# A hybrid decoder layer on one core: TensorE's order in local attention written out by hand, with three branch products moved from its end to its head

## The chip, the core and the metric

The kernel runs on one core of a Trainium2 chip. The metric is the device time of one execution in microseconds (us); the kernel before takes 1939.35 us as the median of three runs (1938.84 to 1944.86). PE is TensorE, ACT is ScalarE, DVE is VectorE, POOL is GpSimd and SP is SyncE, whose queue issues nearly all transfers of this kernel.

## The reference

One decoder layer for 1024 prompt tokens and 8 sample tokens (1032 columns in all), width 1024, in float32. Three branches are computed from one projection of the input, each is projected again by its own 1024 x 1024 matrix, and they are merged by gates:

```python
z = x @ w_in
xr, yr, q, k, v, xq, g = jnp.split(z, SPLIT_IDX, axis=-1)
a_out = hs * gelu(yr)                 # branch a: a gated linear recurrence over xr
s_out = swa_prompt(q, k, v, sinks)    # branch s: window 128, 16 query heads, 4 key/value heads of 64
c_out = mem_attn(xq, mem_k, mem_v)    # branch c: attention into 256 memory tokens
merged = sum(gates[:, :, n] * (br @ w_branch[n]) for n, br in enumerate((a_out, s_out, c_out)))
h = layer_norm(ALPHA * x + merged @ w_out, ...)
h = layer_norm(ALPHA * h + (silu(gt) * up) @ w_down, ...)
```

In `swa_prompt` the tokens lie in 8 blocks of 128. A block's queries see the keys of their own block and of the one before (the first block sees itself alone). Scores are masked to the window, a learned sink per head joins the softmax's sum, and the normalised weights multiply the values.

## The kernel before

The program is built stage by stage: the input projection, the attention into memory (`mem_attention`), local attention (`windows`), what is left of the branch projections, the output projection, the feed-forward block. This case is about `windows` (L634) and what lies at its two ends.

A float32 operand is kept as two parts, high and low, which `split` (L77) makes: ACT casts the high part (L79), DVE subtracts to get the low part (L80). A product is then three matmuls per 128 rows of contraction (`mm3`, L115: high by high, high by low, low by high).

Local attention has 32 steps, one for each of the 4 key/value heads (`kv`) and 8 blocks (`b`). Three groups of work belong to a step:

- `win_scores` (L576): eight matmuls (L594, L595) into two PSUM banks `bs`; DVE adds the mask and finds the maximum (L598), ACT takes the exponential with its sum (L602), DVE the reciprocal (L603), and DVE, POOL and ACT scale the four heads' weights (L607, L609). They lie in the tile `bp`, of which there are three.
- The first half of `win_values` (L612): PE transposes the weights into a bank `bt`, four transposes for each of the one or two key blocks (L619), and `split` makes `bph` and `bpl` of each bank.
- The second half of `win_values`: two matmuls with the values for each key block (L624, L625) into the one bank `bo`; ACT and DVE add its two halves (L629, L630), and SP stores them to the scratch tensor `scr_s` (L632).

`win_load` (L558) loads a head's keys `ks`, queries `st` and values `vs`; there are six `st` tiles for four per head, so the last two of a head take the places of the first two of the head before.

PE has work beside this: the projections of branches a and c. `branch` (L670) is a generator, and each `fill(1)` takes one *branch product* from it (L653), which is 24 matmuls into a bank `bra` or `brc`, for one of 8 row tiles and one of three column ranges c of 384, 390 and 258 columns. There are 24 products for each branch; 11 of branch a are taken in `mem_attention`. `load_branch` (L131) loads a column range of a branch from scratch and splits it; of branch s it is first called behind `windows`, since `scr_s` is what `windows` writes. The products of branch s (`brs`) come next on PE.

The order on every engine is made by a scheduler from the program's order and its own estimate of times, since `windows` writes no order down. In the program's order two products are taken ahead of the first scores, one ahead of each `win_values`, and three are left for the time behind `windows`. PE works through its queue strictly in the order that was set; so do ACT, DVE, POOL and SP with theirs.

Of the kernel before, what the change touches and what calls it, by code (L numbers as in the profile page):

```python
# [18 lines left out]
P = 128  # L19
# [42 lines left out]
class Builder:  # L62
# [546 lines left out]
                (nc.gpsimd if g else nc.vector).tensor_scalar_mul(pg[g], pg[g], r)  # L609
        return pg  # L610

    def win_values(self, kv, ops, b, pg):  # L612
        nc = self.nc
        nk, vs = len(range(max(b - 1, 0), b + 1)), ops[2]
        ov = self.bank("o", f"bo{kv}_{b}")
        for kk in range(nk):
            pt = self.bank("t", f"bt{kv}_{b}_{kk}")
            for g in range(4):
                nc.tensor.transpose(pt[:, g * P:(g + 1) * P], pg[g][:, kk * P:(kk + 1) * P], self.ident)  # L619
            hi = self.ph.tile([P, 512], F32R, tag="pt", name=f"bph{kv}_{b}_{kk}", bufs=4)  # L620
            lo = self.ph.tile([P, 512], F32R, tag="pt", name=f"bpl{kv}_{b}_{kk}", bufs=4)
            self.split(hi, lo, pt)
            v = vs[:, max(b - 1, 0) + kk, :]
            nc.tensor.matmul(ov, v, hi, start=kk == 0, stop=False)  # L624
            self.last_mm = nc.tensor.matmul(ov, v, lo, start=False, stop=kk == nk - 1).ins  # L625
        for i in range(2):
            ob = self.ph.tile([64, 256], F32, tag="ob", name=f"bob{kv}_{b}_{i}", bufs=4)
            o = ov[:, i * 256:(i + 1) * 256]
            nc.scalar.copy(ob, o[64:128, :])  # L629
            nc.vector.tensor_add(ob, o[0:64, :], ob)  # L630
            dst = self.scr["s"][:, 2 * kv + i, b * P:(b + 1) * P].rearrange("(e d) t -> d e t", e=2)
            nc.sync.dma_start(dst, ob.rearrange("p (e t) -> p e t", e=2))  # L632

    def windows(self, fill):  # L634

        self.mask = self.ph.tile([P, 256], F32, tag="mask", name="mask", bufs=1)
        self.nc.sync.dma_start(self.mask, self.io["cst"][:, P:P + 256])
        nxt, last = self.win_load(0), None
        fill(2)
        for kv in range(4):  # L640
            ops = nxt
            for b in range(8):
                pg = self.win_scores(kv, ops, b)
                if last:
                    fill(1)
                    self.win_values(*last)
                last = kv, ops, b, pg
                if b == 4 and kv < 3:
                    nxt = self.win_load(kv + 1)
        fill(1)  # L650
        self.win_values(*last)

    def product(self, step, br, m, c, wb, gate):  # L653

# [958 lines left out]
```

## Time and profile before

| what | value |
|---|---|
| median of three runs | 1939.35 us (1938.84 to 1944.86) |
| the profiled execution | 1941.62 us, of which its instructions span 1939.8 us |
| PE busy | 1902.9 us, 98% of the span |
| DVE, ACT, POOL busy | 72%, 52%, 6% |
| mean granted clock of PE | 0.995 |
| first score matmul of local attention | 825.20 us from the span's start |
| first matmul of branch s | 1046.88 us |

Times in the profile count from the start of the span. A PE instruction's duration is modelled and overlaps the next one's, so what PE really needs for a matmul is read from the distance of two starts, and a PE that is "busy" can still lose time. The names in a row read out<-in. The stage of this change is the stretch of 221.68 us between the last two times of the table.

### The profile page before, as it was taken

What the parts mean: (1) busy time and instruction counts of PE and PEld (TensorE: products, weight loads), DVE (VectorE), ACT (ScalarE), POOL (GpSimd) and SP (SyncE); (2) the same over time, 40 slices, a digit from 0 to 9 for tenths busy, and PEclk for the clock granted to TensorE, in tenths of its full rate; (3) what the DMA queues carried; (4) which work ended last, traced back from release to release, by engine and by line L of the source; (5) the groups of instructions that cost most, each with busy time, mean ns of one, the idle gap of its engine ahead of it and who ended that gap; (6) DMA issues with size and microseconds to landing.
All of it is one profiled execution on the core that took longest, in us unless ns stands there. A gap on an engine that the chain in (4) does not pass through costs nothing.

```text
span 1939.8 us, 37994 instructions
## 1 busy us (share of the span) xinstructions
PE 1902.9 (98%) x14716; PEld 1872.2 (97%) x14716; DVE 1388.3 (72%) x2738; ACT 1001.3 (52%) x2115; POOL 117.1 (6%) x168
## 2 busy tenths in 40 slices
PE   9999999999999999999999999999999999999996
PEld 9999999999999998988899999999999999999996
DVE  7878987887866655378887557785667667858467
ACT  6555565555655544388775224543433434636424
POOL 1000001110000000022210000000000000001001
PEclk9999999999999999999999999999999999999998
DMA  8545555445523376667534352123245245768542
GB/s 318 175 146 168 169 177 180 137 145 204 183 78 127 126 238 212 201 170 209 152 100 148 110 192 71 50 99 98 88 159 191 100 133 181 256 162 231 137 143 88
DMA packets 171637, 303.20 MB, mean 156 GB/s; under 512 B 19568, under 2 KB 86208, under 8 KB 171456
## 3 DMA queue, kind: packets, MB, share of 16 engines
q1 hardware_dynamic: 168384, 290.22, 45.6%
q0 software_dynamic: 3072, 10.55, 2.8%
q8 instruction: 115, 1.88, 0.4%
q14 instruction: 66, 0.54, 0.1%
HBM read 214.79 MB, written 90.09 MB: 157 GB/s over the span
## 4 chain that ended last, share of the span: by engine, by line
PE 86%; ACT 5%; DVE 4%; DMA 3%; issue 1%; ACTq 0%; SPq 0%; DVEq 0%; POOL 0%; POOLq 0%
PE ub L247 5%; PE ub L245 5%; PE ub L246 5%; PE ubfg L245 4%; PE ubfg L246 4%; PE ubfg L247 4%; PE ud L247 3%; PE ud L246 3%; PE ud L245 3%; PE udfg L245 2%; PE udfg L246 2%; PE udfg L247 2%; PE op L122 2%; PE op L120 2%; PE op L121 2%; PE brs L120 2%
## 5 line engine op out<-in xcount | busy, mean ns | idle before, releaser
L122 PE MATMUL op<-mh,wol 128*128 128x258 f32 x256 | 72.3, 282 | 1.3 <-DVE wol L80 1.3
L120 PE MATMUL op<-mh,woh 128*128 128x258 f32 x256 | 72.5, 283 | 0.0
L121 PE MATMUL op<-ml,woh 128*128 128x258 f32 x256 | 72.1, 282 | 0.0
L602 ACT ACTIVATE bp<-bp,bst 128x257 f32<-128x257 f32 (+1 forms) x128 | 62.8, 493 | 17.6 <-DVE bst L598 17.3
L245 PE MATMUL ub<-th,u_4h 128*128 128x258 f32 x240 | 67.8, 283 | 1.3 <-ACT u2s L271 1.3
L245 PE MATMUL ub<-th,u_0h 128*128 128x258 f32 x240 | 68.0, 283 | 0.6 <-ACT zb L1482 0.5
L247 PE MATMUL ub<-th,u_0l 128*128 128x258 f32 x240 | 68.2, 284 | 0.0
L247 PE MATMUL ub<-th,u_4l 128*128 128x258 f32 x240 | 68.2, 284 | 0.0
L247 PE MATMUL ub<-th,u_2l 128*128 128x258 f32 x240 | 68.2, 284 | 0.0
L247 PE MATMUL uc<-th,u_3l 128*128 128x258 f32 x240 | 68.2, 284 | 0.0
L247 PE MATMUL ud<-th,u_1l 128*128 128x258 f32 x240 | 68.2, 284 | 0.0
L247 PE MATMUL ud<-th,u_5l 128*128 128x258 f32 x240 | 68.1, 284 | 0.0
L247 PE MATMUL ub<-th,u_6l 128*128 128x258 f32 x240 | 68.1, 284 | 0.0
L245 PE MATMUL ub<-th,u_6h 128*128 128x258 f32 x240 | 68.0, 283 | 0.0
L245 PE MATMUL uc<-th,u_3h 128*128 128x258 f32 x240 | 67.9, 283 | 0.0
L245 PE MATMUL ub<-th,u_2h 128*128 128x258 f32 x240 | 67.8, 283 | 0.0
L245 PE MATMUL ud<-th,u_5h 128*128 128x258 f32 x240 | 67.8, 282 | 0.0
L245 PE MATMUL ud<-th,u_1h 128*128 128x258 f32 x240 | 67.7, 282 | 0.0
L246 PE MATMUL ub<-tl,u_6h 128*128 128x258 f32 x240 | 67.7, 282 | 0.0
L246 PE MATMUL ud<-tl,u_5h 128*128 128x258 f32 x240 | 67.7, 282 | 0.0
L246 PE MATMUL ub<-tl,u_4h 128*128 128x258 f32 x240 | 67.7, 282 | 0.0
L246 PE MATMUL ud<-tl,u_1h 128*128 128x258 f32 x240 | 67.7, 282 | 0.0
(946 smaller groups left out, 8221.9 us busy)
## 6 DMA issues: line engine op xcount, KB each, us to landing
ur<-win SPq DMA_DIRECT2D x120, 256.0 KB, 3.0
urfg<-wgu SPq DMA_DIRECT2D x80, 256.0 KB, 2.6
scr_f<-G SPq DMA_DIRECT2D x22, 516.0 KB, 3.3
f<-scr_f SPq DMA_DIRECT2D x16, 516.0 KB, 6.1
fs<-scr_t SPq DMA_DIRECT2D x16, 516.0 KB, 8.0
dck<-cmk SPq DMA_DIRECT2D x32, 256.0 KB, 3.5
dcv<-cmvT SPq DMA_DIRECT2D x32, 256.0 KB, 3.4
st<-scr_q SPq DMA_DIRECT2D x32, 256.0 KB, 5.4
```

The costliest lines, as they stand in the source:

```text
L120: nc.tensor.matmul(ps, sh, mh, start=opens and i == 0, stop=False)
L121: nc.tensor.matmul(ps, sh, ml, start=False, stop=False)
L122: self.last_mm = nc.tensor.matmul(ps, sl, mh, start=False, stop=closes and i == last).ins
L245: mm(sh[:, w], xh, start=opens and k == 0, stop=False)
L246: mm(sh[:, w], xl, start=False, stop=False)
L247: self.last_mm = mm(sl[:, w], xh, start=False, stop=k == 3).ins
L602: nc.scalar.activation(x, x, AF.Exp, bias=st[:, g:g + 1], scale=-1.0, accum_out=st[:, 4 + g:5 + g])
```

## The change

`win_values` is cut in two. Its first half becomes `win_turn` (the transposes and their splits), its second half keeps the name. `windows` runs them a step apart and writes PE's order down (`manual_schedule` for PE alone): in each step the scores of block n, the value products of block n-2, the transposes of block n-1, and one whole branch product. Five branch products are taken ahead of the first scores, where two were, so none is left behind the stage. The other engines' orders are still made by the scheduler, which now sees PE's order as given.

```diff
--- before.py
+++ after.py
@@ -609,20 +609,25 @@
                 (nc.gpsimd if g else nc.vector).tensor_scalar_mul(pg[g], pg[g], r)
         return pg
 
-    def win_values(self, kv, ops, b, pg):
-        nc = self.nc
-        nk, vs = len(range(max(b - 1, 0), b + 1)), ops[2]
-        ov = self.bank("o", f"bo{kv}_{b}")
-        for kk in range(nk):
+    def win_turn(self, kv, ops, b, pg):
+
+        out = []
+        for kk in range(2 if b else 1):
             pt = self.bank("t", f"bt{kv}_{b}_{kk}")
             for g in range(4):
-                nc.tensor.transpose(pt[:, g * P:(g + 1) * P], pg[g][:, kk * P:(kk + 1) * P], self.ident)
+                self.nc.tensor.transpose(pt[:, g * P:(g + 1) * P], pg[g][:, kk * P:(kk + 1) * P], self.ident)
             hi = self.ph.tile([P, 512], F32R, tag="pt", name=f"bph{kv}_{b}_{kk}", bufs=4)
             lo = self.ph.tile([P, 512], F32R, tag="pt", name=f"bpl{kv}_{b}_{kk}", bufs=4)
             self.split(hi, lo, pt)
-            v = vs[:, max(b - 1, 0) + kk, :]
+            out.append((ops[2][:, max(b - 1, 0) + kk, :], hi, lo))
+        return kv, b, out
+
+    def win_values(self, kv, b, terms):
+        nc = self.nc
+        ov = self.bank("o", f"bo{kv}_{b}")
+        for kk, (v, hi, lo) in enumerate(terms):
             nc.tensor.matmul(ov, v, hi, start=kk == 0, stop=False)
-            self.last_mm = nc.tensor.matmul(ov, v, lo, start=False, stop=kk == nk - 1).ins
+            self.last_mm = nc.tensor.matmul(ov, v, lo, start=False, stop=kk == len(terms) - 1).ins
         for i in range(2):
             ob = self.ph.tile([64, 256], F32, tag="ob", name=f"bob{kv}_{b}_{i}", bufs=4)
             o = ov[:, i * 256:(i + 1) * 256]
@@ -635,20 +640,25 @@
 
         self.mask = self.ph.tile([P, 256], F32, tag="mask", name="mask", bufs=1)
         self.nc.sync.dma_start(self.mask, self.io["cst"][:, P:P + 256])
-        nxt, last = self.win_load(0), None
-        fill(2)
-        for kv in range(4):
-            ops = nxt
-            for b in range(8):
-                pg = self.win_scores(kv, ops, b)
-                if last:
-                    fill(1)
-                    self.win_values(*last)
-                last = kv, ops, b, pg
-                if b == 4 and kv < 3:
-                    nxt = self.win_load(kv + 1)
-        fill(1)
-        self.win_values(*last)
+        nxt, scored, turned = self.win_load(0), None, None
+        fill(5)
+        with self.tc.manual_schedule(engines={mybir.EngineType.PE}):
+            for kv in range(4):
+                ops = nxt
+                for b in range(8):
+                    pg = self.win_scores(kv, ops, b)
+                    if turned:
+                        self.win_values(*turned)
+                    if scored:
+                        turned = self.win_turn(*scored)
+                        fill(1)
+                    scored = kv, ops, b, pg
+                    if b == 4 and kv < 3:
+                        nxt = self.win_load(kv + 1)
+            self.win_values(*turned)
+            turned = self.win_turn(*scored)
+            fill(1)
+            self.win_values(*turned)
 
     def product(self, step, br, m, c, wb, gate):
```

Every engine keeps its instructions, and their number; only their order differs. On PE it is the same up to the last three matmuls of the product `bra5_0`, and again from the first matmul of branch s.

The first place is the head of the stage on PE, where the first transposes stand (`bt0_0_0` and `bp0_0` belong to head 0, block 0; the number behind a name is the buffer's). Before:

```order
L594 MATMUL bs0_3_0_11199<-ks0_0_10929,st0_0_10935 128x256
L619 MATMUL bt0_0_0_11094<-ident_63,bp0_0_11016 128x128
L595 MATMUL bs0_3_0_11199<-ks0_1_10930,st0_0_10935 128x256
L619 MATMUL bt0_0_0_11094<-ident_63,bp0_0_11016 128x128 x2
L594 MATMUL bs0_3_0_11199<-ks0_0_10929,st0_1_10938 128x256
L619 MATMUL bt0_0_0_11094<-ident_63,bp0_0_11016 128x128
L595 MATMUL bs0_3_0_11199<-ks0_1_10930,st0_1_10938 128x256
```

Now:

```order
L594 MATMUL bs0_1_1_11145<-ks0_0_10929,st0_2_10941 128x256
L595 MATMUL bs0_1_1_11145<-ks0_1_10930,st0_2_10941 128x256
L594 MATMUL bs0_1_1_11145<-ks0_0_10929,st0_3_10944 128x256
L595 MATMUL bs0_1_1_11145<-ks0_1_10930,st0_3_10944 128x256
L618 MATMUL bt0_0_0_11161<-ident_63,bp0_0_11110 128x128 x4
L120 MATMUL bra5_1_11170<-baH0_1_9710,wba50_h_11071 128x390
L121 MATMUL bra5_1_11170<-baL0_1_9711,wba50_h_11071 128x390
L122 MATMUL bra5_1_11170<-baH0_1_9710,wba50_l_11072 128x390
```

The first transposes stood among the scores of block 3, taken apart by them; now they stand right behind the scores of block 1 and ahead of the next branch product.

The second place is the end of the stage on PE, from the last transposes or the last branch product (`brc7_2`) on; `bo3_7` is the value product of the last block, `brs0_0` the first product of branch s. Before:

```order
L619 MATMUL bt3_7_1_13949<-ident_63,bp3_7_13827 128x128 x4
L120 MATMUL brc7_0_14026<-bcH0_0_12020,wbc70_h_14016 128x384
L121 MATMUL brc7_0_14026<-bcL0_0_12021,wbc70_h_14016 128x384
L624 MATMUL bo3_7_13937<-bph3_7_0_13943,vs3_12939 128x512
L122 MATMUL brc7_0_14026<-bcH0_0_12020,wbc70_l_14017 128x384
L120 MATMUL brc7_0_14026<-bcH1_0_12023,wbc70_h_14016 128x384
L121 MATMUL brc7_0_14026<-bcL1_0_12024,wbc70_h_14016 128x384
L625 MATMUL bo3_7_13937<-bpl3_7_0_13944,vs3_12939 128x512
L624 MATMUL bo3_7_13937<-bph3_7_1_13954,vs3_12939 128x512
L122 MATMUL brc7_0_14026<-bcH1_0_12023,wbc70_l_14017 128x384
L625 MATMUL bo3_7_13937<-bpl3_7_1_13955,vs3_12939 128x512
```

Now:

```order
L120 MATMUL brc7_2_14025<-bcH7_2_12354,wbc71_h_13879 128x258
L121 MATMUL brc7_2_14025<-bcL7_2_12355,wbc71_h_13879 128x258
L122 MATMUL brc7_2_14025<-bcH7_2_12354,wbc71_l_13880 128x258
L629 MATMUL bo3_7_14052<-bph3_7_0_14012,vs3_13023 128x512
L630 MATMUL bo3_7_14052<-bpl3_7_0_14013,vs3_13023 128x512
L629 MATMUL bo3_7_14052<-bph3_7_1_14021,vs3_13023 128x512
L630 MATMUL bo3_7_14052<-bpl3_7_1_14022,vs3_13023 128x512
L120 MATMUL brs0_0_14144<-bsH0_0_14070,wbs00_h_14134 128x384
L121 MATMUL brs0_0_14144<-bsL0_0_14071,wbs00_h_14134 128x384
L122 MATMUL brs0_0_14144<-bsH0_0_14070,wbs00_l_14135 128x384
```

The last value product stood four matmuls into `brc7_0`, with the rest of that product, `brc7_1` and `brc7_2` behind it; now it is the last thing ahead of branch s.

The third place is SP's queue at the same point: the last stores of `scr_s` (from the tiles `bob3_7`), the loads of branch s (`bsL`), weight loads (`wbs`) and a gate load (`gts`, 128 x 1032). Before:

```order
L632 DMA scr_s_73<-bob3_6_1_13906 64x2x128
L680 DMA gts0_14127<-scr_g_75 128x1032
L95 DMA wbs3r1__14524<-wbr 128x512
L632 DMA scr_s_73<-bob3_7_0_13960 64x2x128
L632 DMA scr_s_73<-bob3_7_1_13964 64x2x128
L138 DMA bsL0_0_13973<-scr_s_73 128x384
L138 DMA bsL1_0_13976<-scr_s_73 128x384
```

Now:

```order
L95 DMA wbs4r0__14624<-wbr 128x512
L95 DMA wbs4r1__14630<-wbr 128x512
L637 DMA scr_s_73<-bob3_7_0_14057 64x2x128
L690 DMA gts1_14173<-scr_g_75 128x1032
L637 DMA scr_s_73<-bob3_7_1_14061 64x2x128
L138 DMA bsL0_0_14071<-scr_s_73 128x384
L138 DMA bsL1_0_14074<-scr_s_73 128x384
```

The loads of branch s stand right behind the last store in both. The gate load (now that of the next row tile, `gts1`) has moved from ahead of the last two stores to between them, and two weight loads stand ahead of both where there was one.

## The prediction

> **What bounds the kernel now.** I read the page's head first, then the stretches of the stage, then PE's instructions one by one.
>
> ```profile
> span 1939.8 us, 37994 instructions
> PE 1902.9 (98%) x14716; PEld 1872.2 (97%) x14716; DVE 1388.3 (72%) x2738; ACT 1001.3 (52%) x2115; POOL 117.1 (6%) x168
> ```
>
> PE bounds the whole span. The change moves PE's instructions and drops none, so it can give back only time that PE loses between them. The stretches of the stage (columns: length; busy time with instructions of PE, weight loads, DVE, ACT, POOL; granted clock; DMA share; GB/s):
>
> ```profile
> 825.20:836.00 10.80, 10.80 (x77) 10.80 (x77) 4.77 (x19) 3.61 (x13) 0.00 (x0) 1.00 0.99 241
> 836.00:980.00 144.00, 138.49 (x886) 126.30 (x886) 125.25 (x391) 120.34 (x365) 31.79 (x48) 1.00 0.62 173
> 980.00:1022.00 42.00, 41.71 (x273) 39.30 (x272) 33.16 (x100) 29.61 (x89) 8.64 (x13) 1.00 0.28 78
> ```
>
> PE's busy time hides its losses, because durations overlap. So I price each kind by distances of starts:
>
> ```profile
> 844.43 0.40 PE L624 MATMUL bo<-bph,vs 128*128 128x512 f32 x1
> 844.66 0.39 PE L625 MATMUL bo<-bpl,vs 128*128 128x512 f32 x1
> 844.89 0.82 PE L619 MATMUL bt<-ident,bp 128*128 128x128 f32 x6
> 845.67 0.28 PE L595 MATMUL bs<-ks,st 128*128 128x256 f32 x1
> 845.78 0.29 PE L594 MATMUL bs<-ks,st 128*128 128x256 f32 x1
> ...
> 1039.70 0.34 PE L120 MATMUL brc<-bcH,wbc_h 128*128 128x390 f32 x1
> 1043.99 0.28 PE L120 MATMUL brc<-bcH,wbc_h 128*128 128x258 f32 x1
> 1046.88 0.34 PE L120 MATMUL brs<-bsH,wbs_h 128*128 128x384 f32 x1
> 1051.04 0.34 PE L120 MATMUL brs<-bsH,wbs_h 128*128 128x384 f32 x1
> ```
>
> A value matmul takes 0.234 (844.43 to 844.89, two), a score matmul 0.118, and six transposes with one score matmul 0.78, so a transpose 0.11. A branch product of 24 matmuls takes 4.29 for 390 columns, 2.89 for 258 and 4.16 for 384. By the code the stage holds 11 products of each width less 21 matmuls of one (43 + 47 + 32 us), 224 score matmuls (26), 32 of half size (2), 240 transposes (26) and 120 value matmuls (28): 203.6 us in a stretch of 221.7. **PE loses 18.1 us here**, and that is the most the change can return. Most of it lies in 836 to 980, where DVE and ACT are busy 87% and 84% of the time. Who waited for the split weights shows the kind:
>
> ```profile
> PEld bo L624: 8.8, 26
> PE bo L624: 2.4, 5
> PEld bo L625: 1.7, 6
> ```
>
> 12.9 us were spent by value products on splits whose transposes stood only a little ahead of them.
>
> **The change part by part.** *The steady steps.* A step on PE is now scores (0.94), values (0.94), transposes (0.88) and a product: 6.9, 7.1 or 5.7 us. Between a block's transposes and its value product lie a product and a block's scores, 3.8 to 5.2 us. Two casts and two subtractions of 0.6 to 0.7 us each must fit in it beside the engine's other work, so those 12.9 us should go. DVE and ACT fit on average: in the 196.8 us of the three rows they are busy for 163 and 154. What is late next: the scores' way to the next transposes. Its length is seen at the last block, from the last score matmul to POOL's scaling:
>
> ```profile
> 1023.89 0.28 PE L595 MATMUL bs<-ks,st 128*128 128x256 f32 x1
> 1027.05 1.09 POOL L609 TENSOR_SCALAR bp<-bp,bst 128x256 f32<-128x256 f32 x1 [5.24 <-DVE bst L603]
> ```
>
> That is 4.0 us undisturbed, and the new order leaves 7.9 (6.6 where the product is the narrow one). From 836 to 980 PE stood visibly idle for 5.5 us (144.0 less 138.5), in the quieter 980 to 1022 for 0.3. For the whole interior I leave 1.5, nearer to the quiet row; bounds 0.5 and 5.5. On SP some stores now stand behind weight loads; only the four `bob` tiles wait for stores, two steps later, so I cost that at nothing (a step's length at most where two stores are late together, inside the 5.5).
>
> *The head.* The same products stand ahead of the first scores as before, but now nothing may be put between these scores and the first transposes except block 1's scores. First the loads:
>
> ```profile
> 812.75 2.64 SPq L566 DMA_DIRECT2D ks<-scr_k  x4
> 815.45 5.21 SPq L570 DMA_DIRECT2D st<-scr_q  x8
> 820.00:840.00 20.00, 20.00 (x139) 19.64 (x138) 10.26 (x41) 8.85 (x29) 1.68 (x3) 1.00 0.80 196
> DMA to landing us min/median/max: 3.7/5.4/9.6
> ```
>
> Twelve loads of 256 KB, 3.15 MB at 196 GB/s, land by about 828.4 (the last, issued by 820.7, lands between 824 and 830 by the last row, which is that of `st`). PE reaches block 0's scores at 825.7, three held-back matmuls later than before. They end at 828.5, the chain of a half-size block takes about 3 (an estimate from the 4.0), and the first transposes start near 831.3. PE has 1.4 us of scores to do in these 5.6 (some transposes start sooner): **3.9 us lost**, bounds 2.0 (loads there at once) and 5.5.
>
> *The changes of head.* The last two `st` of a head take places that are free when the last block's scores have read them. At the change from the third to the fourth head:
>
> ```profile
> 967.85 0.36 PE L594 MATMUL bs<-ks,st 128*128 128x256 f32 x1
> 968.37 2.40 SPq L570 DMA_DIRECT2D st<-scr_q  x4
> ```
>
> The fourth issue comes 2.3 us behind the scores' start and lands 5.4 later: 7.7. Before, products filled this time. Now the next scores need it when a step and two score matmuls have passed: at 7.3 and 7.1 at the first two changes, at 6.0 at the third, whose product is narrow: 0.4 + 0.6 + 1.7 = **2.7 us lost**. Bounds 0 (at 3.7 each) and 5 (weight loads stand ahead of the second pair on SP, and wait for a place of their own).
>
> *The end.* The three products that followed the last value product are gone to the head. Behind it stands a chain that they covered:
>
> ```profile
> 1036.35 0.39 PE L625 MATMUL bo<-bpl,vs 128*128 128x512 f32 x1
> 1038.03 0.42 DVE L630 TENSOR_TENSOR bob<-bo,bob 64x256 f32<-64x256 f32 x1 [0.44 <-ACT bob L629]
> 1039.15 7.54 SPq L138 DMA_DIRECT2D bsL<-scr_s  x15
> DMA to landing us min/median/max: 2.6/4.4/4.8
> 1041.77 1.00 ACT L79 CAST bsH<-bsL 128x384 fp32r<-128x384 f32 x2 [3.77 <-DMA bsL<-scr_s]
> 1042.32 0.56 DVE L80 TENSOR_TENSOR bsL<-bsL,bsH 128x384 fp32r<-128x384 f32 x1 [1.27 <-ACT bsH L79]
> 1043.83 1.01 ACT L79 CAST bsH<-bsL 128x384 fp32r<-128x384 f32 x2 [1.05 <-DMA bsL<-scr_s]
> 1040.00:1050.00 10.00, 10.00 (x66) 10.00 (x65) 7.38 (x16) 6.49 (x15) 0.00 (x0) 1.00 0.90 300
> ```
>
> From the last value matmul's end (1036.74) to the first load's issue: 2.4, with the gate load now between the last stores 2.8. The first load lands 2.6 later, its cast and subtraction take 1.05: at 6.45 the first of eight row tiles is ready. A tile is 0.197 MB: 0.66 us at the 300 GB/s of the last row, 1.03 by the casts (two at 1041.77, the third waiting until 1043.83). I take 0.75, near the bandwidth. The eighth is ready at 11.7, its three matmuls end at 12.2, and the product itself is worth 4.16: **8.1 us lost**; bounds 7.1 (at 0.66, the gate load costing nothing more) and 11.8 (at 1.03, plus its 528 KB ahead, 1.8).
>
> *The clock.* Idle PE lost its clock twice near here:
>
> ```profile
> 696.60 0.44 PE L121 MATMUL bra<-baL,wba_h 128*128 128x384 f32 x1 [2.05 <-DVE baL L80]
> 697.11:700.52 3.41, 3.41 (x13) 3.41 (x12) 3.41 (x8) 0.71 (x2) 0.00 (x0) 0.50 0.78 265
> 763.80 0.39 PE L120 MATMUL cs<-mkh,cqh 128*128 128x256 f32 x1 [1.37 <-ACT cp L507]
> 765.38:768.79 3.41, 3.41 (x14) 3.02 (x13) 3.34 (x8) 1.78 (x6) 0.00 (x0) 0.50 0.70 228
> ```
>
> After gaps of 2.05 and 1.37 us it ran at half speed for 3.41. The head's gap (two pieces of near 2 and 1) should do the same: 1.1 of the 1.7 us that this costs at most if it happens once, bounds 0 and 2. At the end the first half-speed product is paced by its loads anyway: 1.0, bounds 0 and 2.
>
> [...]
>
> **The sum.** Lost before 18.1; lost after 1.5 + 3.9 + 2.7 + 8.1 + 1.1 + 1.0 = 18.3. Net +0.2 (all lower ends together: 9.6 lost, 8.5 faster; all upper ends: 31.8, 13.7 slower). The profiled execution took 1941.62 us around its span of 1939.8, 2.3 above the median of the runs; the same +0.2 on the median 1939.35 gives **1939.6 us**. What the steps gain, the two ends take back.
>
> **The rivals.** *Slower: the vector engines can't hold the written tempo.* Before, a late block let other PE work pass; now PE stands. The nine steps from head 0, block 6 on also carry branch c's 24 casts and subtractions, on engines already busy 84 and 87% there. If casts that wait for their loads sit ahead of exponentials in ACT's queue, the way from scores to transposes grows from 4.0 past the 6.6 to 7.9 that the order leaves; from that point each further us is paid in every step. One us over in nine steps: 9 more, 1948.6. Against it: the slack of 2.6 to 3.9 us. *Faster: the head and the changes stay clean.* If loads land at their shortest, the losses are 2.0 + 0 + 0.5 at the head and inside, with an end of 7.1 and its clock 1.0: 10.6, so 7.5 gained, 1931.9. Against it: the DMA share of 0.99 at the stage's start. *The end at its long bound*, 3.7 more: 1943.3. That PE's order might not be what the change says is excluded by the order itself.
>
> **How the numbers follow.** Balance 0.45 (1935 to 1944), long end 0.20, slow tempo 0.22, clean head 0.13. 0.3% is 5.8 us, about what a measurement of this kernel can tell from no change. The first two lie within it (0.65), slow tempo is slower (0.22), clean head faster (0.13). The range leaves out a tenth at each side: 1932.5 to 1948.
>
> **What would show it.** Right: in the new profile `bo` L629 and L630 wait for almost nothing; the first `brs` matmul stands about 6.5 us behind the last `bo`, with `bsL` loads as its releaser through the splits; the first `bt` waits some us for POOL or ACT; the granted clock drops to 0.5 once or twice between 826 and 1045. Wrong: PE waits in steps 7 to 15 on `bp` or `bph` (slow tempo), or a gap of under 4 us ahead of `brs`, which would mean that loads of branch s start before the last store.

## The result and the profile after

The changed kernel takes 1953.41 us in the median of five runs (1951.64 to 1956.13), the kernel before 1939.35 (1938.84 to 1945.04): a ratio of **1.0064**, 95% interval 1.0053 to 1.0075. Run once more beside the experiments (e6 below) it took 1952.93 us, a ratio of 1.0052 (1.0036 to 1.0068). The change makes the kernel about 0.6% slower; the forecast was 1939.6, with a range that ended at 1948.

The head of the page of the changed kernel (its profiled execution took 1951.64 us):

```profile
span 1949.9 us, 38019 instructions
PE 1900.6 (97%) x14716; PEld 1874.4 (96%) x14716; DVE 1389.0 (71%) x2738; ACT 1005.2 (52%) x2115; POOL 114.4 (6%) x168
```

PE, DVE, ACT and POOL have the same number of instructions, PE's busy time is even 2.3 us less, and the span is 10.1 us longer. By this count the difference is PE standing; what half clock costs lies inside the busy time (matmuls of `bra` with 390 columns start 0.325 us apart from 832.24 to 835.49, at half clock, and 0.18 from 835.81 to 837.79, at full) and does not show here. Where PE stands, shows the list of who waited for whom on PE in the stage, 820 to 1062 us (total us, times, longest):

```profile
PE brs L120 <- ACT bsH L79: 7.8, 1, 7.8
PE bs L594 <- DMA st<-scr_q: 6.9, 6, 1.8
PE brc L121 <- DVE bcL L80: 1.8, 3, 1.3
PE bt L618 <- DVE bp L609: 0.9, 1, 0.9
```

The value products (`bo`) are not in it. This list is of PE alone, and most of the 12.9 us of before were rows of its weight loads (PEld), of which one is left now (total us, times):

```profile
PEld bo L630: 0.5, 2
```

So these waits are gone, as forecast. But 12.9 was too much: before, each of the five PE waits (2.4 us) begins at the same moment as a PEld wait, and counted once they are the 10.5 us of the PEld rows. In their place stand the end of the stage (`brs`), the query loads (`st`) and a little of branch c's splits. The stretches of the stage (length; busy time of PE, weight loads, DVE, ACT, POOL; granted clock; DMA share; GB/s) confirm it:

```profile
823.63:838.00 14.37, 10.09 (x46) 9.40 (x46) 4.94 (x22) 5.71 (x21) 1.84 (x3) 0.76 0.91 239
870.00:886.50 16.50, 14.68 (x91) 13.76 (x90) 13.15 (x40) 13.01 (x39) 2.22 (x4) 0.90 0.76 209
942.70:986.70 44.00, 44.00 (x303) 42.59 (x303) 36.86 (x115) 33.61 (x101) 9.08 (x14) 1.00 0.52 142
994.70:1034.00 39.30, 39.30 (x267) 38.07 (x267) 32.87 (x101) 29.68 (x87) 7.32 (x11) 1.00 0.28 76
1034.00:1053.71 19.71, 11.94 (x79) 10.98 (x78) 10.64 (x28) 9.01 (x24) 1.09 (x1) 0.93 0.40 119
828.97:835.79 6.82, 5.95 (x20) 5.68 (x21) 3.12 (x13) 4.50 (x17) 1.84 (x3) 0.50 1.03 260
880.17:883.58 3.41, 3.41 (x15) 2.93 (x13) 1.51 (x8) 2.38 (x11) 0.70 (x1) 0.50 0.86 273
1050.83:1057.66 6.83, 3.95 (x11) 3.65 (x12) 3.97 (x8) 4.34 (x9) 0.00 (x0) 0.50 1.03 357
```

Rows 3 and 4 are the steady steps: PE is busy for all of their 44.0 and 39.3 us. Rows 1, 2 and 5 are the head, the first change of head and the end, with 4.3, 1.8 and 7.8 us of standing. The last three rows are all the half clock that the stage has: 17.1 us of it, each piece at or directly behind one of these three places. The kernel before had none inside the stage. PE's own rows at the head and the change of head (start, length, instruction, idle time before it and who ended it):

```profile
825.56 0.30 PE L594 MATMUL bs<-ks,st 128*128 128x128 f32 x1 [1.37 <-DMA st<-scr_q]
827.80 0.30 PE L594 MATMUL bs<-ks,st 128*128 128x128 f32 x1 [1.83 <-DMA st<-scr_q]
831.03 1.09 PE L618 MATMUL bt<-ident,bp 128*128 128x128 f32 x4 [0.87 <-DVE bp L609]
878.42 0.30 PE L594 MATMUL bs<-ks,st 128*128 128x128 f32 x1 [0.77 <-DMA st<-scr_q]
879.89 0.30 PE L594 MATMUL bs<-ks,st 128*128 128x128 f32 x1 [1.06 <-DMA st<-scr_q]
```

And the end, from the last value product to branch s's first:

```profile
1045.54 0.40 PE L630 MATMUL bo<-bpl,vs 128*128 128x512 f32 x1
1048.13 0.58 SPq L637 DMA_DIRECT2D scr_s<-bob  x1
1048.81 11.30 SPq L138 DMA_DIRECT2D bsL<-scr_s  x22
1053.14 7.17 ACT L79 CAST bsH<-bsL 128x384 fp32r<-128x384 f32 x14 [5.95 <-DMA bsL<-scr_s]
1053.71 0.69 PE L120 MATMUL brs<-bsH,wbs_h 128*128 128x384 f32 x1 [7.77 <-ACT bsH L79]
```

The load goes out 0.7 us behind the last store, its cast starts 4.3 us later, and the first product another 0.6 behind. Its matmul lasts 0.69 us where a row of before shows 0.34: half clock. Twenty-four of them take 6.2 us (1053.71 to 1059.92) in place of 4.16.

**A yardstick.** The whole times of two runs of one kernel differ by some us (the five of the changed kernel by up to 4.5). So I compare versions by one distance on PE too, called W: from the tenth product of branch a to the third of branch s. The same work lies between these two in every version. Before:

```profile
789.23 0.34 PE L120 MATMUL bra<-baH,wba_h 128*128 128x384 f32 x1
1055.20 0.34 PE L120 MATMUL brs<-bsH,wbs_h 128*128 128x390 f32 x1
```

After:

```profile
787.14 0.34 PE L120 MATMUL bra<-baH,wba_h 128*128 128x384 f32 x1
1064.08 0.34 PE L120 MATMUL brs<-bsH,wbs_h 128*128 128x390 f32 x1
```

W is 266.0 before and 276.9 after: **11.0 us more**, the whole difference of the two profiled executions (10.0) within 1.

### The profile page after: what moved, and what is told of

It is laid out like the page before. It is cut to its first block, busy times and chain, and to the rows that moved or that the text cites. A ratio compares the mean times of both kernels' runs of the same rounds, so it can differ in the third digit from the quotient of the medians.

```text
span 1949.9 us, 38019 instructions
## 1 busy us (share of the span) xinstructions
PE 1900.6 (97%) x14716; PEld 1874.4 (96%) x14716; DVE 1389.0 (71%) x2738; ACT 1005.2 (52%) x2115; POOL 114.4 (6%) x168
## 4 chain that ended last, share of the span: by engine, by line
PE 85%; DMA 7%; DVE 4%; ACT 2%; issue 1%; SPq 1%; ACTq 0%; DVEq 0%; POOL 0%; POOLq 0%
PE ub L247 5%; PE ub L245 5%; PE ub L246 5%; PE ubfg L245 4%; PE ubfg L246 4%; PE ubfg L247 4%; PE ud L247 3%; PE ud L246 3%; PE ud L245 3%; PE udfg L245 2%; PE udfg L246 2%; PE udfg L247 2%; PE brs L120 2%; PE brs L121 2%; PE brs L122 2%; PE ubf L245 2%
## 5 line engine op out<-in xcount | busy, mean ns | idle before, releaser
L120 PE MATMUL brs<-bsH,wbs_h 128*128 128x384 f32 (+2 forms) x192 | 62.4, 325 | 7.8 <-ACT bsH L79 7.8
```

The lines of the kernel that those rows point to most:

```text
L120: nc.tensor.matmul(ps, sh, mh, start=opens and i == 0, stop=False)
```

## The experiments

The expectations name theories: A, PE's standing at the two ends and at the changes of head, with half clock behind it, is the loss, and the new order gains inside; B, the three products moved from the end are all of it; C, the written order is too tight for the vector engines. D and E come up where they are tested. Times are medians; each ratio is to the kernel before on the same chip, whose own median there was 1940.6 to 1942.7 us. e1 to e4 ran on one chip, e5, e6, b1 and b2 on a second, c1 to c3 on a third and d1 on a fourth, so runs of different groups are better compared by ratio or by W than by their times.

| run | what it is | us | ratio (95%) | W |
|---|---|---|---|---|
| before | | 1939.35 | 1 | 266.0 |
| changed | | 1953.41 | 1.0064 (1.0053 to 1.0075) | 276.9 |
| e6 | changed, again | 1952.93 | 1.0052 (1.0036 to 1.0068) | 277.8 |
| e1 | before, five ahead | 1948.48 | 1.0032 (1.0020 to 1.0045) | 275.0 |
| e2 | changed, two ahead | 1951.05 | 1.0047 (1.0034 to 1.0059) | 274.9 |
| e3 | changed, six ahead | 1947.39 | 1.0030 (1.0019 to 1.0041) | 273.4 |
| e4 | changed, st in halves | 1944.17 | 1.0012 (1.0003 to 1.0021) | 270.0 |
| e5 | changed, gaps filled (too much) | 1952.43 | 1.0052 (1.0040 to 1.0065) | 273.7 |
| c3 | changed, gaps filled (less) | 1950.34 | 1.0040 (1.0026 to 1.0054) | 272.7 |
| d1 | changed, order written from head 1 | 1946.78 | 1.0028 (1.0019 to 1.0037) | 270.9 |
| c1 | changed, order not written | 1941.92 | 0.9998 (0.9987 to 1.0009) | 265.9 |
| b1 | e4, branch s early | 1936.20 | 0.9966 (0.9954 to 0.9978) | 260.8 |
| b2 | b1, order not written | 1932.02 | **0.9943** (0.9931 to 0.9955) | 257.1 |
| c2 | b2 with before's order of the code | 1939.66 | 0.9987 (0.9976 to 0.9998) | 266.0 |

The stretches of W in which versions differ, in us between starts of PE's instructions: from the first score matmul of one block to that of another (block 0 to 31), then from the last value product's end to branch s's first matmul, and that product's own length. The number of branch products in each is the same for all of these:

| | 0 to 7 | 7 to 10 | 10 to 15 | 15 to 18 | 18 to 23 | 23 to 26 | gap at the end | first brs product |
|---|---|---|---|---|---|---|---|---|
| changed | 46.4 | 22.9 | 34.6 | 20.3 | 33.2 | 20.2 | 7.8 | 6.2 |
| e6 | 47.5 | 22.8 | 34.7 | 19.7 | 33.1 | 20.4 | 7.5 | 6.5 |
| e5 | 46.1 | 20.5 | 36.2 | 19.6 | 33.2 | 20.9 | 7.5 | 4.5 |
| c3 | 45.0 | 21.5 | 35.2 | 19.6 | 33.2 | 20.3 | 8.0 | 4.7 |
| e4 | 40.9 | 20.6 | 38.0 | 19.1 | 33.2 | 19.1 | 7.1 | 6.8 |
| d1 | 39.8 | 21.3 | 38.0 | 19.6 | 33.1 | 20.3 | 7.2 | 6.3 |
| c1 | 39.8 | 20.2 | 34.5 | 19.8 | 33.1 | 19.1 | 7.0 | 7.2 |
| b1 | 42.3 | 20.4 | 36.5 | 19.1 | 33.1 | 19.1 | 0.1 | 4.9 |
| b2 | 39.5 | 19.9 | 35.9 | 19.4 | 33.1 | 19.1 | 0.1 | 4.9 |

**e6: the changed kernel again**, as a reference for the runs beside it.

> The changed kernel once more, on the chip and in the rounds of the other runs, as their reference. Expected 1951 to 1955, a ratio of 1.005 to 1.007 to the kernel before.

It did, and its stretches agree with the first execution's within 1.1 us each. The half clock does not repeat so well: here it lasts 10.24 us from 827.50, 3.41 from 882.11 and 10.24 from 1049.37, 23.9 us in all against 17.1, behind nearly the same gaps. W is 0.8 longer.

**e1, e2: one half of the change at a time.** e1 is before's code with `fill(5)` for `fill(2)`, e2 the changed code with the opposite edit.

```diff
-        fill(2)
+        fill(5)
```

> Before's code and the scheduler's own order, but five products ahead of the first scores and none left behind the last value product. Theory A (the loss is PE standing at the stage's ends and at the changes of head, each gap dear because half clock follows it; the written order by itself gains inside): the uncovered end as in the changed kernel, 7.8 us idle and 2.0 of half clock, on top of what before loses inside (18.1): 1939.4 + 9.8 = 1949, between 1946 and 1952, so 2 to 7 us faster than the changed kernel only if the scheduler's head stays clean. Theory B (the three moved products explain all of it, the written order does nothing): like the changed kernel, 1953 to 1955. Theory C (the written order itself is too tight for the vector engines): less than half of the loss, at most 1944.

> The written order with two products ahead of the first scores, so that three are left behind the last value product as before. Theory A: the end is covered (9.8 us less than the changed kernel), but PE stands in front of the first scores until their loads are there, the three products' 11.3 us longer than now: 1953.4 - 9.8 + 11.3 = 1955, between 1951 and 1958, with waits on st and ks of some 15 us around the head and none ahead of brs. Theory B: the time comes back, 1940 to 1944. Theory C: 1951 to 1955, with steps longer than 7.1 us throughout.

e1, at 1948.5 us, lies in A's range and outside those of B and C; e2, at 1951.05, at the lower edge of A's. Moving the products alone costs 6 us (0.32%), less than the change. With the products back at the end e2 shows no wait ahead of `brs`, but 14.5 us for `st` in place of 6.9: what the end gives back, the head takes, since PE comes to the first scores before their loads do. Theory B's 1940 to 1944 for e2 is refuted. e2's time alone would fit C too, but C also asked for steps longer than 7.1 us throughout, and from block 18 to 23 e2's five steps take 33.8 us, 6.8 each.

**e3: one product more at the head.** `fill(6)`, so that none is left between the last transposes and the last value product.

> The written order with six products ahead; the product between the last transposes and the last value product is the one that is missing then. Theory A: the first scores come 4.2 us later, so their loads are there: the head's 8.1 us fall to 1 to 2 (the wait for the first softmax stays), while the last value product waits some 2.5 us for its split: 1953.4 - 6.5 + 2.5 = 1949, between 1947 and 1951. Theory B: one more product taken from the end makes it slower, 1956 to 1958. Theory C: no change beyond the 2.5 us, 1955 to 1956.

1947.4, against B and C. PE's waits in it:

```profile
PE brs L120 <- ACT bsH L79: 5.6, 1, 5.6
PE bs L594 <- DMA st<-scr_q: 5.4, 4, 2.1
PE bo L629 <- DVE bob L635: 2.0, 1, 2.0
```

The 2.0 is the uncovered last value product. None of the 5.4 us for `st` lies at the head any more, only at the changes; first score to the third block's fell from 14.3 to 7.5 us. So the head's loads were late by less than one product.

**e4: the query tiles in halves.** `st` becomes two tags of four tiles of 512 columns; the second half of a head is loaded behind its first scores, the first half of the next head as soon as block 3 is scored.

```diff
-            st = ph.tile([P, TP], F32R, tag="st", name=f"st{kv}_{g}", bufs=6)
...
+            st = self.ph.tile([P, TP // 2], F32R, tag=f"st{h}", name=f"st{h}_{kv}_{g}", bufs=4)
```

> The changed kernel, with the query tiles st in halves of four blocks each, loaded half by half (the second half of a head only behind its first scores): no load of a next head waits for the last scores of this one, and the first scores wait for half as many query bytes. Theory A: the idle time at the three changes (1.8 + 0.9 + 0.9) and the half clock behind the first (1.7) go, 5.4 us; at the head one to four us of the waits on loads and of the half clock go as well: 1953.4 - 5.4 - 2.5 = 1945.5, between 1943 and 1949. Theory B: only the end counts, 1952 to 1954. Theory C: the waits move into the steps, 1951 to 1954.

1944.2, as A said: the waits for `st` are gone at the head and at all three changes (by the table 5.5 + 2.3 + 1.2 + 1.1 us). But 3.4 us are given back between blocks 10 and 15, where PE now comes too early for branch c's splits:

```profile
PE brs L120 <- ACT bsH L79: 7.1, 1, 7.1
PE brc L121 <- DVE bcL L80: 2.9, 3, 1.5
```

**e5, c3: what the half clock costs.** Products of no use, read by nobody, keep PE busy in its gaps: before the second and third query tile's first scores, before the first transposes, and behind the last value product. c3 is e5 with 10, 14 and 6 small ones in place of 22, 28 and 12.

```diff
...
+            warm = self.bank("t", "warmw")
+            for _ in range(30):
+                self.nc.tensor.matmul(warm, v, hi, start=True, stop=True)
```

> The changed kernel with small products of no use put where TensorE stands: 22 and 28 of 128x128 before the second and third query tile's first scores, 12 before the first transposes, 30 of 128x512 (7 us) behind the last value product. Their results are read by nobody; the kernel computes what it did. Theory A: the waits stay, but no half clock follows them: 3.5 us less at the head and 2.0 less at the end, 1953.4 - 5.5 = 1948, between 1946 and 1950.5, with the first branch-s product near 4.2 us instead of 6.2. If the half clock cost nothing (the products behind the gaps are paced by their splits anyway): 1953 to 1955.

> The changed kernel with products of no use in its gaps once more, now shorter than the gaps: 10, 14 and 6 of 128x128 (0.112 us each in the last such run, where 22, 28 and 12 overran the gaps by some 2.8 us) and 30 of 128x512 behind the last value product. Theory A: the head falls from 14.3 to 15.4 us (first scores to third block's scores) to 11 to 12, branch s's first product from 6.2 to 4.5: 1953 - 5.5 = 1947.5, between 1946 and 1950. If half clock is not what costs there: 1952 to 1954.

The end of e5, and the first of its fillers at the head:

```profile
1045.28 7.16 PE L674 MATMUL warmw<-bph,vs 128*128 128x512 f32 x30
1052.89 0.61 PE L120 MATMUL brs<-bsH,wbs_h 128*128 128x384 f32 x2 [0.46 <-ACT bsH L79]
```

```profile
824.56 2.62 PE L581 MATMUL warmh<-ones 128*128 128x128 f32 x22
```

At the end the effect is plain: with the same gap, the first product takes 4.5 and 4.7 us in place of 6.2 and 6.5, so the half clock there costs 1.7 us and more. The head was a poor experiment: a filler takes 0.112 us (2.46 us from 824.56 to the next score matmul at 827.02, for 22), twice what I had reckoned, and e5's overran the gaps by about 2.8 us, which ate the gain. In c3 they were short, the gaps stayed partly open, and one of the two half-clock pieces of 3.41 us came back, at 830.19. As whole runs both lie between the ranges of their two theories: e5 (1952.4) can't be told from the changed kernel (e6), and c3 is 2.6 us under e6 where 5.5 were expected, with intervals that overlap. In W e5 is 3.2 us below the changed kernel in spite of its overrun, and its granted clock is 1.00 both at the head (824.39 to 838.45) and over the gap at the end (1045.44 to 1052.89). That half clock costs some us is shown; how much of the head's 8 us is its share follows only from the rows above.

**d1, c1: who may move PE's instructions.** c1 is the changed kernel with nothing else than

```diff
-        with self.tc.manual_schedule(engines={mybir.EngineType.PE}):
+        with nullcontext():
```

and d1 lifts it for the first head only.

> The changed kernel with its order not written down: the same code and so the same order of priorities, but the scheduler may move TensorE's instructions. In its list only the head differs much: branch products stand between the single scores of blocks 0 to 3; behind block 7 of the first head both orders are nearly the same. Theory A, as mended by the last runs (the loss of the written order is its head, the gain comes from the new order of the code): the head's 8.1 us shrink to 1 to 2, the rest stays: 1953 - 6.5 = 1946.5, between 1944 and 1949. Theory D (the written order also costs in the steady steps): under 1944. Theory E (the written order is what brings the steady steps' gain): 1951 or more.

> The changed kernel with the written order from the second head on only; the first head's TensorE instructions are the scheduler's. It parts the 11 us between the changed kernel and the same code free of the written order. Theory A: the head's share, 7 us from the first scores to block 7's (46.4 to 47.5 us with the written order, 39.8 without), comes back, while the waits at the changes of head stay: 1953 - 7 = 1946, between 1944 and 1948.5, with the stretch over the first change of head near 22.9 us again. If the changes of head carry most of it: 1949 to 1952. If the whole 11 us are the head's: 1941 to 1943.

c1: 1941.9 us, 0.9998 of before, and **all of the 11 us are gone** from W. That is 2 us below A's bounds, on the side of D; but D's place is wrong, since blocks 18 to 23 take the same 33.1 us in both. In c1's rows at the head a product stands where the written order had PE wait:

```profile
826.07 0.22 PE L594 MATMUL bs<-ks,st 128*128 128x128 f32 x1
826.13 0.28 PE L595 MATMUL bs<-ks,st 128*128 128x128 f32 x1
826.24 0.39 PE L120 MATMUL bra<-baH,wba_h 128*128 128x390 f32 x1
...
828.44 0.23 PE L594 MATMUL bs<-ks,st 128*128 128x128 f32 x1
```

and the first 14 us have no gap, and full clock (the columns of the stretches above):

```profile
826.00:840.00 14.00, 14.00 (x101) 13.68 (x99) 8.29 (x37) 7.27 (x26) 1.69 (x3) 1.00 0.86 212
```

Its value products wait for 1.2 us in all, 0.2 of it for a cast. So it is the order of the code, values two blocks behind the scores, that brings the steady steps' gain, and not its being written down. e1 against c1 says the same, since they differ in the order of the code alone (both free, both with five products ahead): W is 275.0 and 265.9, 9.1 us apart, and in e1 weight loads of value products wait 29 times for casts, 11.6 us in all (in c1 once, 0.5). One limit stays: where PE is free, the scheduler makes the other engines' orders anew too, and no run parts the two.

Where the 11 us went: against the changed kernel c1 has 6.6 us less at the head (46.4 to 39.8) and 2.7, 0.5 and 1.1 us less at the three changes; its end is about the same in all. d1 brings back the 6.6 of the head. d1 then waits 3.0 us for branch c's splits, as e4 does (blocks 10 to 15 take 38.0 us, in c1 34.5), and that is the largest part of what still divides it from c1; so its 1946.8 is the 7 us that A gave, made of 6.6 and 1.6 at the first change gained, 1.1 in small things at the later stretches and the end, and 3.4 given back: 5.9 (6.1 in W).

**b1, b2, c2: the end mended.** Branch s's first 384 columns need only blocks 0 to 2 of each head. In b1 (on top of e4) they are loaded into tiles of their own while the last head still runs, and their splits come ahead of the last block's copies in the code. The eight new tiles take 12 KB a partition, 8 KB of which the halves of `st` set free.

```diff
+    def load_early(self):
+        self.lo_s = [self.slot("L", 0, f"bsL{k}_0", True) for k in range(KT)]
+        for k, lo in enumerate(self.lo_s):
+            self.nc.sync.dma_start(lo.bitcast(F32), self.scr["s"][:, k, :CH[0][1]])
...
+                    if b == 4 and kv == 3:
+                        self.load_early()
```

b2 lifts the written order from b1; c2 also puts the code back into before's order (a block's product, transposes and values together).

> The kernel with st in halves, and with branch s's first 384 columns loaded into tiles of their own while the last head still runs; their splits stand ahead of the last block's copies. The written order and five products ahead stay. Theory A: the end's gap of 7.1 us and the half clock behind it (2.6) go: 1944.2 - 9.7 = 1934.5, between 1932 and 1938, which is faster than both kernels; the first brs matmul within 1.5 us of the last value product, steps as before. Theory B: the same, since it also puts the loss at the end, but then with st whole it would have been enough. Theory C: the extra loads and splits in the last steps stretch them: 1938 to 1944.

> The same kernel (st in halves, branch s's first columns early, five products ahead) without the written order: the scheduler orders TensorE. This prices the order by itself, with both ends mended. Theory A: the value products wait for their splits again as with five ahead and the free order (5 us and more), 2 to 8 us slower than with the written order: 1937 to 1943. Theory C: as fast or faster than with the written order, at most 1934.5.

> Before's order of the code (a block's product, transposes and value products together, one block behind the scores), free for the scheduler, with everything else as in the fastest run: st in halves, branch s's first columns early, five products ahead. It prices the change's order alone, with both ends mended. Theory A: the value products wait for their splits again, 5 to 11 us: 1932 + 5 to 11 = 1937 to 1943. If the mended ends and loads were all: 1930 to 1934.

The end in b2, a load of branch s and PE's rows:

```profile
1015.78 0.33 SPq L136 DMA_DIRECT2D bsL<-scr_s  x1
```

```profile
1040.85 0.40 PE L647 MATMUL bo<-bpl,vs 128*128 128x512 f32 x1
1041.32 0.62 PE L121 MATMUL brs<-bsH,wbs_h 128*128 128x384 f32 x2
1042.24 0.45 PE L122 MATMUL brs<-bsL,wbs_h 128*128 128x384 f32 x1 [0.30 <-DVE bsL L81]
```

The last load is issued 25 us before it is needed, and the gap is 0.1 us. b1 is 8.0 us faster than e4 (9.7 expected, 9.2 in W), and faster than before. b2's expectation missed: I had the written order 2 to 8 us ahead, and it is 4 us behind. The time is the one that theory C gave (at most 1934.5), but not for C's reason: blocks 18 to 23 take 33.1 us in b1 and in b2, and 2.8 of the 3.7 us in W lie in blocks 0 to 7, the head, as c1 then showed. **b2 is the fastest version, 0.57% faster than before.** c2 prices the order of the code with everything else equal: 7.6 us more than b2 (8.8 in W). Who waited for the cast weights in c2:

```profile
PEld bo L646: 10.8, 31
PE bo L646: 4.1, 10
```

In b2 no `bo` waits for casts at all; two wait for subtractions:

```profile
PEld bo L647: 2.0, 4
PE bo L647: 0.5, 2
```

## Why the prediction was wrong, point by point

The lost time of the changed kernel, worked out as in the prediction (a stretch less its work at full clock; the profiled execution):

| term | forecast | measured |
|---|---|---|
| steady steps and the rest of the interior | 1.5 | 3.8 |
| head, with its clock | 3.9 + 1.1 | 8.1 (4.3 standing, 3.8 clock and rest) |
| changes of head | 2.7 | 7.3 (3.7 standing, 3.6 clock and rest) |
| end, with its clock | 8.1 + 1.0 | 7.8 + 2.1 |
| sum | 18.3 | 29.1 |

29.1 less the 18.1 of before is the 11.0 of W.

*The value products* were right: two weight loads wait 0.5 us for a split, where the rows of before had 10.5 (given as 12.9, with 2.4 counted twice; the sum does not use the 12.9). *The steady steps* were right: 44.0 and 39.3 us without a gap. *The rest of the interior* was 2.3 too small: a stretch of 13.6 us from 914.0 lost 2.3, most of it in `brc` waiting for splits of branch c's third column range (1.6 us). This is the place of the rival "slow tempo" but not its mechanism: a branch product waited for its own splits, no transpose waited there, and it never became one per step.

*The standing itself* came out near in its totals: 4.3 us at the head against 3.9, 3.7 at the changes against 2.7, 7.8 at the end against 8.1. Only the head is right as it was reasoned: its transposes start at 831.03, forecast 831.3. (3.15 MB at 196 GB/s from 812.75 on end at 828.8, not at the prediction's 828.4; the last wait for these loads ended at 827.80.)

The end is luck. The 8.1 was 6.45 until the first row tile was ready and 1.6 of waiting for the other seven inside the product. Measured, PE stood for 7.8 us, since the first load took 4.3 us where 2.6 stood, and then the product had no gap: in e5, at full clock, it takes 4.5 us in place of 4.16. The errors nearly cancel.

The changes were forecast as 0.4, 0.6 and 1.7 us, the third the worst; they were 1.8, 0.9 and 0.9. At the first one the late loads were issued later behind the last block's first scores than at the other two (1.8 us, 870.04 to 871.85, against 0.8 and 0.4), in SP's queue right behind two loads of branch c (870.71). The four issues,

```profile
871.85 2.41 SPq L570 DMA_DIRECT2D st<-scr_q  x4
```

stand together at all three changes. The last of them landed 6.1 us behind its issue, and the first scores of the next head waited until 878.42 and 879.89.

**The step that failed is the clock.** Its term was mis-sized. It was priced at 1.1 behind the head, "if it happens once", 1.0 at the end, and nothing at the changes. It happened at three places, for 6.8, 3.4 and 6.8 us. At the head PE came back (831.03) in the middle of one 3.41 us piece of half clock and ran through a second one (to 835.79), with half of a branch product (12 of its 24 matmuls) at half speed in it; the first change had been given no clock at all. At the end the 1.0 rested on the product's being paced by its loads, which it was not. PE was busy for 5.95, 3.41 and 3.95 us of these pieces. If full clock had halved all of it, the clock cost 3.0 + 1.7 + 2.0 = 6.7 us where 2.1 stood: an estimate from the last three rows of the stretches, and an upper one, since the starts of `bra` matmuls lie 0.325 us apart there and 0.18 behind, 1.8 times. That is up to 4.6 (3.8 by the factor of 1.8) of the 10.8 us by which the sum was short, the largest single error. The rest of the interior is 2.3 of it and the standing 1.1; the 2.8 to 3.6 that are left, small terms in the table's "clock and rest", are not parted further. e5 and c3 show that the half clock at the end goes when PE is kept busy; at the head it is the rows, not an experiment, that part standing and clock.

The gaps behind which the clock fell at the head and the first change were short: no single one was longer than 1.83 us. The pieces of 3.41, 6.82 and 6.83 us are once and twice the 3.41 us of each drop in the kernel before.

**What the sum did not ask** is who could have filled the gaps. The prediction took the written order as the cause of the gain inside and priced the head and the changes as standing that the new order brings. c1 shows that the gain belongs to the order of the code and the standing to its being fixed: fixed order and gain could be had apart. The balance that I forecast (+0.2) is nearly what c1 has (W 265.9 against 266.0), where PE may fill its gaps: there the end takes back what the steps gain. That is another kernel, so it does not bear the forecast out. The written order adds 11 us of its own on top. The rivals "clean head" and "long end" did not come: the end took 9.9 in all against 9.1. Most of the signs that the prediction named for being right came all the same (no `bo` standing on PE, two drops of the clock before 1045): they tell the mechanism and not the sizes.

The median's difference to before, 14.1 us, is above the profiled executions' 10.0. The profiled execution is the fastest of its five, with a granted clock of 0.991 where the others have 0.988 to 0.990; in the repeat the difference of the medians is 10.3 (1952.93 less 1942.67). I take the rest for the clock elsewhere in the program and have not settled it.

## What to carry to other kernels

Change the order of the code first, and fix an engine's order only where that gains something by itself. Here it gained nothing (blocks 18 to 23 take 33.2 us fixed and 33.1 free), and it cost where transfers decide, above all at a stage's first steps: the same order of the code took 11 us more in W when it was fixed, and 3.7 us more with both ends mended (b1 against b2). When work that covers a chain is moved away, shorten the chain first: loading what the next stage needs first, as soon as its part is stored, took the end's gap from 7 us to 0.1. And price a gap on TensorE with the half clock behind it, not by its length alone: at the head 6.8 us of half clock went with 4.3 us of standing.

## What the runs showed of the hardware

The granted clock fell behind gaps far shorter than the 3.41 us of a half-clock piece: 0.77 + 1.06 us of standing within 2.2 us were enough (the first change of head), single gaps of 0.93 us at the two later changes were not. The starts of the pieces lie whole multiples of 3.41 us apart: 15 from 828.97 to 880.17, 50 from there to 1050.83. In the 3.41 us right ahead of each, PE was busy for 1.38, 1.59 and 0.00 us. The longest gap alone does not part the cases: single gaps of 1.37 and 1.27 us (ahead of 825.56 and 919.99) kept the clock, and 0.77 + 1.06 lost it. Nor does the busy time within such a length: stretches with 2.04 and 1.93 us of it (from 822.15 and 1044.01) kept the clock, and in the kernel before one with 2.04 (from 761.97) lost it. What the clock goes by these rows do not settle.

In the stage the pieces were 3.41, 6.83 or 10.24 us long (the last in c1 from 1040.05, around a gap of 7.0 us, and in e1, e3, e4 and e6), and 17.07 in e2 from 815.54, where PE stood for 8.7 us and four more times, and the first branch product behind a gap at the end took between 4.5 us (PE kept busy) and 7.4 us (e3).

Winning time early in the stage was partly lost again at one place: in d1 and e4 blocks 10 to 15 took 38.0 us in place of 34.6, as the splits of branch c did not come earlier with PE (PE waited 3.0 and 2.9 us for them).
